# Moving the group-0 scores of a dilated attention layer six chunks later in its period

## The chip, the cores and the metric

The kernel runs on one core of a Trainium2 chip. The core has five engines with queues of their own: TensorE (PE in the profile, with its weight loads as PEld), VectorE (DVE), ScalarE (ACT), GpSimd (POOL) and SyncE (SP, which here only issues DMAs). They share the on-chip memory SBUF; PE writes its sums into the eight banks of PSUM, from which DVE and ACT read. The metric is the device time of one execution in microseconds. Times are medians of several runs; a profile is one more execution, recorded instruction by instruction.

## The reference

The program is a two-layer encoder trunk over 512 tokens of 1024 features, in float32. Layer 0 is a windowed attention, layer 1 a dilated one; each is followed by a SwiGLU feed-forward block. The change lies in layer 1's attention:

```python
DILATED_GROUPS = ((128, 1), (512, 4), (2048, 16))   # (window, dilation)

def dilated_mixture_attention(h, w_qkv, w_out):
    qkv = (h @ w_qkv).reshape(b, s, N_GROUPS_B, 3, H_B, HEAD_DIM)
    for gi, (win, dil) in enumerate(DILATED_GROUPS):
        q, k, v = (to_residue(qkv[:, :, gi, i], dil) for i in range(3))
        o, lse = banded_attention(q, k, v, slopes, dil, win // (2 * dil), BLOCK_B)
        outs.append(from_residue(o)); lses.append(from_residue(lse))
    wts = softmax(stack(lses), axis=0)
    o = einsum('gbsh,gbshd->bshd', wts, stack(outs))
    return o.reshape(b, s, H_B * HEAD_DIM) @ w_out
```

Each of 16 heads has queries, keys and values of its own in each of three groups. A group's scores are scaled, biased by distance, masked to a band, put through a softmax and multiplied with the values; the groups' results are then weighted by their softmax denominators and added.

## The kernel before

**Products.** A float32 operand is split into a high and a low part of the type that PE multiplies fast (ACT copies the high part, DVE subtracts it from the operand, lines 92 to 94), and a product is made of three: high by high, high by low, low by high (`mm3`, line 117). Weights are split in the same way when they arrive, `wh` by ACT and `wl` by DVE, in tiles of three buffers.

**Fillers.** Layer 1 needs, for each pair of heads (p from 0 to 7) and each group (0, 1, 2), a unit of queries, a unit of keys and a share of values. These products have few dependencies and are used as filling: the generator `fillers` (line 1276) lines all of them up, and each `next(fill)` issues one **chunk**, which is always six products of 128x256 (one eighth of a query or key unit, one sixteenth of a value unit). A unit of queries or keys is eight chunks in one of the three PSUM banks `mm`; at its end DVE scales it into SBUF (lines 1006 and 1017). For group 0 the result is split further: `split_queries` (line 129) makes the tiles `qs`, `split_keys` (line 134) the tiles `ks` and `kl`, with copies on ACT (lines 136, 137, 139) and a subtraction on DVE (line 138).

In each pair's period of 64 chunks the fillers come in this order: queries and keys of groups 1 and 2 of pair p (four units, 32 chunks), group 0's queries of pair p+1 (8), a unit of values (16), group 0's keys of pair p+1 (8). Pair 0 has 16 chunks more, a further unit of values ahead of the queries of pair 1. `spread([4], fill)` ahead of the loop lets the fillers run four chunks ahead, so that the keys of group 0 for pair p are over four chunks before the period of pair p begins.

**Attention.** Between the chunks stand the steps of attention itself. For group 0 (`attention_a`):

- `scores_a` (line 1045) for query blocks 0 and 1, then for 2 and 3: eight products each into the two banks `sc` (line 1063), then the bias, mask and maximum on DVE (line 1071) and the exponential on ACT (line 1076).
- `merge` (line 1187): POOL sends the softmax statistics to DRAM with two DMAs and reads them back in another order with four (lines 1192 to 1198).
- `turn_a` (line 1079), once per query block: PE transposes the probabilities into a bank `tp`; ACT or DVE copies them to SBUF (`evacuate`).
- `weigh`, called **the burst** here: without a chunk in between, PE issues the value products of groups 1 and 2 of the pair before (`finish`, line 1177, whose sum DVE adds at line 1183), those of group 0 of this pair (`weigh_a`, lines 1100 and 1104), and the scores of groups 1 and 2 (`scores_b`, line 1122). `scores_b` brings DVE work (lines 1135 to 1150), exponentials on ACT (line 1142) and a scaling on POOL (line 1154).

After the burst `attention_b` gives two transposes of groups 1 and 2 (`turn_b`, line 1164) and the merging rows (line 1204).

**Order.** PE's order is the order of the program (line 70: a schedule by hand for PE). In this layer the order of the other engines' instructions is laid out by the planner when the program is built, and each engine then works strictly in it.

**Where the steps stand.** `weave` (line 157) spreads `total` chunks evenly over the list that `attention_a` returns; a number in that list counts as a step of its own (and asks for that many chunks besides, here 0). The list has 13 entries, so entry i stands after `total * i // 13` chunks. With 32 chunks (pairs 1 to 7) the steps stand after 0 (first scores), 4 (second scores), 9 (merge), 12, 14, 17 and 22 (transposes) and 29 chunks (burst); three chunks more follow. With 48 chunks (pair 0) they stand after 0, 7, 14, 18, 22, 25, 33 and 44 chunks; four more follow. Then come 13 chunks, `first` (the transposes of the burst's first half), 8 chunks, `second`, 4 chunks, `rows`, 7 chunks. In the last pair it is 8 chunks, `first`, 5 chunks, `second`, `rows`, 2 chunks, and the fillers of its second half are parts of the output projection (`out_part`).

Of the kernel before, what the change touches and what calls it, by code (L numbers as in the profile page):

```python
# [66 lines left out]
def trunk(ctx, tc, xT, gains, sink, tabs, qsc, wunits, wv, outT, outR):  # L67
# [10 lines left out]
    def bank(tag, name=None):  # L78
        return psum.tile([128, 512], F32, tag=tag, name=name or tag, bufs=BUFS[tag])
# [73 lines left out]
    def chain(*gens):  # L153
        for _, g in gens:
            yield from g

    def weave(main, fill, total):

        done = 0
        for i, step in enumerate(main):  # L160
            want = total * (i + 1) // len(main)
            spread([step, want - done], fill)
            done = want

    def spread(main, fill):

        for step in main:
            if callable(step):
                step()
            else:  # L170
                for _ in range(step):
                    next(fill)
# [158 lines left out]
    with tc.tile_pool(name="l0", bufs=2) as pool:  # L331
# [7 lines left out]
        def k_unit(P, **kw):  # L339
            def done(ps):  # L340
                t = spool.tile([128, S], F32, name="tmp")
                nc.vector.tensor_tensor(t, ps, norm["rb"], op=OP.mult)
                qk["k", P] = [pool.tile([128, S], F32R, name=f"kt{a}") for a in range(2)]
                qk["kl", P] = [pool.tile([128, S], F32R, name=f"kl{a}") for a in range(2)]
                split_keys(t, qk["k", P], qk["kl", P])
            return unit(5 * P, xh, xl, "mm", done, **kw)

        def q_unit(P, i, **kw):
            def done(ps):
                t = spool.tile([128, S], F32, name="tmp")  # L350
                col = 4 * P + i
                nc.vector.scalar_tensor_tensor(t, ps, qs_sb[:, col:col + 1], norm["rb"], op0=OP.mult, op1=OP.mult)
                qk["q", P, i] = apart(pool, any(k[0] == "q" for k in qk), lambda: [
                    pool.tile([128, S], F32R, name=f"qt{a}", bufs=8) for a in range(2)])
                split_queries(t, qk["q", P, i])
            return unit(5 * P + 1 + i, xh, xl, "mm", done, **kw)
# [96 lines left out]
        def out_part(j, lo, hi, w={}):  # L453
            def gen():
                if lo == 0:
                    w[j] = load_unit(wunits[10 + j], (NK, 128))
                    out_ps[j] = bank("mm")
                wh, wl = w[j]
                for c in range(lo, hi):
                    mm3(out_ps[j], wh[:, c], wl[:, c], oh[:, c, :], ol[:, c, :], c == 0, c == NK - 1)  # L460
                    if c == NK - 1:
                        residual(j, out_ps[j], 1)
                    yield
            return hi - lo, gen()
# [4 lines left out]
        fill = chain((16, early), q_unit(0, 2), q_unit(0, 3), k_unit(1),  # L469
                     *[q_unit(1, i) for i in range(4)],  # L470
                     *[out_part(j, 0, 4) for j in range(3)], *[out_part(j, 4, 6) for j in range(3)])
# [509 lines left out]
    with tc.tile_pool(name="l1", bufs=2) as pool:  # L981
# [58 lines left out]
        def tile_a(t):  # L1040


            return 256 * (t % 2), 256 if t else 128

        def scores_a(p, ts):
            if ts[0] == 0:

                st["sta", p] = pool.tile([128, 4, 4], F32, name="sta")
            sta = st["sta", p]
            ps = [bank("sc") for a in range(2)]  # L1050
            pr = st["pr", p, ts] = pool.tile([128, 2, 512], F32, name="pr1", bufs=2)
            for t in ts:
                o = tile_a(t)[0]
                for a in range(2):
                    out, kp = ps[a][:, o:o + 256], [qk[n, p][a] for n in ("ks", "kl")]
                    if t == 0:

                        out = out.rearrange("p (b k) -> p b k", b=2)
                        kp = [k.rearrange("p (b k) -> p b k", b=4)[:, 0::3, :] for k in kp]
                    else:  # L1060
                        kp = [k[:, 128 * t - 128:128 * t + 128] for k in kp]
                    for k in range(2):
                        nc.tensor.matmul(out, qk["qs", p][a][:, 128 * t:128 * t + 128], kp[k],  # L1063
                                         start=t == ts[0] and k == 0, stop=k == 1, skip_group_check=True)
            for t in ts:
                o, n = tile_a(t)
                mx = pool.tile([128, 2], F32, name="mx1", bufs=4)
                for a in range(2):
                    for rows, at, tb in ((slice(0, 128), o, taba),) if t else ((HALVES[0], o + 128, tabe),
                                                                              (HALVES[1], o, tabe)):  # L1070
                        nc.vector.tensor_tensor_reduce(
                            out=pr[rows, a, o:o + n], in0=ps[a][rows, at:at + n], in1=tb[rows],
                            scale=SLOPES[2 * p + a], scalar=-3e38, op0=OP.add, op1=OP.max, accum_out=mx[rows, a:a + 1])
                nc.vector.tensor_scalar(sta[:, t, 0:2], mx, -1.0, None, op0=OP.mult)
                for a in range(2):
                    nc.scalar.activation(pr[:, a, o:o + n], pr[:, a, o:o + n], AF.Exp, bias=sta[:, t, a:a + 1],
                                         accum_out=sta[:, t, 2 + a:3 + a])

        def turn_a(p, ts, t):
            o, n = tile_a(t)  # L1080
            nb = n // 128
            tp = bank("tp")
            for a in range(2):
                for kb in range(nb):
                    nc.tensor.transpose(tp[:, (nb * a + kb) * 128:(nb * a + kb) * 128 + 128],  # L1085
                                        st["pr", p, ts][:, a, o + 128 * kb:o + 128 * kb + 128], ident)
            pt = st["pt"] = pool.tile([128, 512], F32, name="pt1", bufs=8)
            evacuate(pt[:, :2 * n], tp[:, :2 * n], t)
            return pt
# [97 lines left out]
        def merge(p):  # L1187


            sta = st["sta", p]  # L1190
            by_query = dram.tile([S + 64, 4], F32, name="stats")
            nc.gpsimd.dma_start(by_query[:S].rearrange("(t q) e -> q t e", t=4), sta)
            nc.gpsimd.dma_start(by_query[S:], sta[:64, 0, :])

            sa = st["sa", p] = pool.tile([128, 4, 4], F32, name="sa")
            by_class = by_query[64:].rearrange("(m c i) e -> i m c e", c=4, i=4)
            for i in range(4):
                nc.gpsimd.dma_start(sa[32 * i:32 * i + 32], by_class[i])
# [9 lines left out]
        def attention_a(p):  # L1208

            pts = {}  # L1210

            def turn(ts, t):
                pts[t] = turn_a(p, ts, t)

            def weigh():

                if p:
                    finish(p - 1)
                for t in range(4):
                    weigh_a(p, t, pts[t])  # L1220
                scores_b(p, (0, 1))
                scores_b(p, (2, 3))

            return [lambda: scores_a(p, (0, 1)), 0, lambda: scores_a(p, (2, 3)), 0,
                    lambda: merge(p), lambda: turn((0, 1), 0), lambda: turn((0, 1), 1),
                    lambda: turn((2, 3), 2), 0, lambda: turn((2, 3), 3), 0, 0, weigh]

        def attention_b(p):
            def turn(cs):
                st["pts", p, cs[0]] = turn_b(p, cs)  # L1230

            return [lambda: turn((0, 1)), lambda: turn((2, 3)), lambda: merge_rows(p)]

        def finish(p):
            for c in range(4):
                weigh_b(p, c, st["pts", p, c // 2 * 2])
# [58 lines left out]
        fill = fillers()  # L1295
        spread([4], fill)
        for p in range(8):
            weave(attention_a(p), fill, 48 if p == 0 else 32)
            first, second, rows = attention_b(p)
            if p < 7:  # L1300
                spread([13, first, 8, second, 4, rows, 7], fill)
# [99 lines left out]
```

## Time and profile before

| | us |
|---|---|
| runs | 1426.27, 1424.46, 1425.81 |
| median | 1425.81 |
| profiled execution | 1426.05 |
| its span, first to last instruction | 1424.3 |

| engine | busy us | share of the span |
|---|---|---|
| DVE | 857.0 | 60% |
| ACT | 683.5 | 48% |
| POOL | 232.0 | 16% |

Layer 1's attention with its fillers lies between about 582 and 1042 us of the span. A row of a timeline gives the start, the duration, engine, line, operation, and what is written and read (out<-in); a number in square brackets is the idle time of the engine just before, with the instruction that ended it. A row of a window gives the stretch, its length, the busy time and count of PE, PEld, DVE, ACT and POOL, then the granted share of PE's clock, the busy share of the DMA engines and GB/s. The busy time of a product on PE includes a tail that the next product overlaps, so that a chain of products is measured from start to start.

### The profile page before, as it was taken

To read this page: it belongs to the slowest core of one execution; us is meant where nothing else is said; L and a number is where in the kernel's file an instruction comes from. 1 tells how busy PE (TensorE), PEld (TensorE's weight loads), DVE (VectorE), ACT (ScalarE), POOL (GpSimd) and SP (SyncE) were. 2 spreads that over 40 slices of the span, in tenths; PEclk is the share of its full clock that TensorE was granted. 3 is DMA by queue.
4 is the path that set the end of the run, shared out by engine and by line. 5 is a ranking of instruction groups with operands and counts; after the bars stand their busy time and mean duration, and the time that the engine had idled before them with its cause. 6 is when DMAs were issued, how large, how long until landed. Compare 5 with 4: busy or idle time off the path is not lost. (4 is left out here: it accounts for less than half of the span.)

```text
span 1424.3 us, 29674 instructions
## 1 busy us (share of the span) xinstructions
PE 1398.5 (98%) x12418; PEld 1377.5 (97%) x12418; DVE 857.0 (60%) x1581; ACT 683.5 (48%) x1247; POOL 232.0 (16%) x325
## 2 busy tenths in 40 slices
PE   8999999999999999999999999999999999999998
PEld 8898999999999999999999999999999999999998
DVE  6776568843786373445554555546556884478733
ACT  6776434632565265344544445445443463256522
POOL 4334220100110120111121101111122010011022
PEclk9999999999999999999999999999999999999999
DMA  6110262833772232322122222122126284378121
GB/s 199 60 46 31 90 178 90 216 112 117 202 191 65 96 110 90 105 72 93 61 76 75 75 76 75 61 90 75 61 89 178 90 209 116 121 196 197 65 97 71
DMA packets 60486, 153.62 MB, mean 108 GB/s; under 512 B 8256, under 2 KB 13632, under 8 KB 60352
## 3 DMA queue, kind: packets, MB, share of 16 engines
q1 hardware_dynamic: 49168, 134.26, 28.3%
q0 software_dynamic: 10752, 16.92, 7.5%
q8 instruction: 97, 1.59, 0.4%
q10 hardware_dynamic: 432, 0.54, 0.1%
q14 instruction: 37, 0.30, 0.1%
HBM read 149.52 MB, written 2.17 MB: 107 GB/s over the span
## 5 line engine op out<-in xcount | busy, mean ns | idle before, releaser
L94 DVE TENSOR_TENSOR wl<-wraw,wh 128x1024 fp32r<-128x1024 f32 (+4 forms) x192 | 214.2, 1119 | 174.6 <-ACT wh L93 173.1
L93 ACT ACTIVATE wh<-wraw 128x1024 fp32r<-128x1024 f32 (+4 forms) x192 | 181.3, 949 | 265.2 <-PE mm L122 165.2
L122 PE MATMUL mm<-xh,wh 128*128 128x256 f32 x1320 | 270.6, 285 | 1.1 <-ACT wh L93 1.1
L122 PE MATMUL mm<-xh,wl 128*128 128x256 f32 x1320 | 263.2, 280 | 2.1 <-DVE wl L94 2.1
L122 PE MATMUL mm<-xl,wh 128*128 128x256 f32 x1320 | 263.1, 280 | 0.0
L122 PEld LDWEIGHTS mm<-xh,wh 128*128 128x128 f32 x1320 | 204.0, 191 | 3.7 <-issue 1.5
L122 PEld LDWEIGHTS mm<-xh,wl 128*128 128x128 f32 x1320 | 203.2, 191 | 2.7 <-DVE wl L94 2.5
L122 PEld LDWEIGHTS mm<-xl,wh 128*128 128x128 f32 x1320 | 203.4, 191 | 0.0
L653 POOL DMA_DIRECT2D w<-wunits x64 | 56.0, 917 | 416.5 <-DMA w<-wunits 111.9
L255 POOL TENSOR_TENSOR ssum<-ssum,tmp 128x512 f32<-128x512 f32 x33 | 54.1, 1639 | 191.9 <-ACT tmp L252 129.9
L122 PE MATMUL psv<-wh,xh 128*128 128x256 f32 x288 | 81.1, 281 | 0.0
L122 PE MATMUL psv<-wh,xl 128*128 128x256 f32 x288 | 80.3, 279 | 0.0
L122 PE MATMUL psv<-wl,xh 128*128 128x256 f32 x288 | 80.2, 279 | 0.0
L696 PE MATMUL mm<-bh,wh 128*128 128x256 f32 x256 | 70.7, 276 | 0.0
L696 PE MATMUL mm<-bl,wh 128*128 128x256 f32 x256 | 70.7, 276 | 0.0
L696 PE MATMUL mm<-bh,wl 128*128 128x256 f32 x256 | 70.7, 276 | 0.0
L696 PE MATMUL sc<-bh,wh 128*128 128x256 f32 x256 | 70.7, 276 | 0.0
L696 PE MATMUL sc<-bl,wh 128*128 128x256 f32 x256 | 70.7, 276 | 0.0
L696 PE MATMUL sc<-bh,wl 128*128 128x256 f32 x256 | 70.7, 276 | 0.0
L696 PE MATMUL mm<-bh,h 128*128 128x256 f32 x256 | 70.7, 276 | 0.0
L696 PE MATMUL mm<-bl,h 128*128 128x256 f32 x256 | 70.7, 276 | 0.0
L696 PE MATMUL mm<-bh,l 128*128 128x256 f32 x256 | 70.7, 276 | 0.0
(240 smaller groups left out, 3718.6 us busy)
## 6 DMA issues: line engine op xcount, KB each, us to landing
wraw<-wunits SPq DMA_DIRECT2D x159, 512.0 KB, 3.3
w<-wunits SPq DMA_DIRECT2D x96, 256.0 KB, 4.3
w<-wunits POOLq DMA_DIRECT2D x64, 256.0 KB, 5.8
wraw<-wv SPq DMA_DIRECT2D x25, 512.0 KB, 3.3
wraw<-wunits SPq DMA_DIRECT2D x28, 192.0 KB, 2.4
x<-xT SPq DMA_DIRECT2D x8, 256.0 KB, 4.9
wraw<-wunits SPq DMA_DIRECT2D x4, 256.0 KB, 4.9
wraw<-wunits SPq DMA_DIRECT2D x2, 384.0 KB, 2.9
```

The lines of the kernel that those rows point to most:

```text
L93: nc.scalar.activation(out_h, src, AF.Copy)
L94: nc.vector.tensor_tensor(out_l, src, out_h.bitcast(F32), op=OP.subtract)
L122: nc.tensor.matmul(out[:, cols], a, b[:, cols], start=first and k == 0 and c == 0, stop=last and k == 2, skip_group_check=True)
L255: nc.gpsimd.tensor_tensor(norm["sum"], norm["sum"], sq, op=OP.add)
L653: nc.gpsimd.dma_start(sums[:, 512 * k:512 * k + 512], v[:, 0:512], accum_op=OP.add)
L696: nc.tensor.matmul(out, a[:, j], b[:, j], start=first and j == 0 and i == 0, stop=j == 3 and i == 2, skip_group_check=True)
```

## The change

The spreading by `weave` is replaced by numbers of chunks written into the list. They are 6 chunks (22 for pair 0) ahead of the first scores, and then 4, 5, 2, 2, 4, 3 and 6.

```diff
-            return [lambda: scores_a(p, (0, 1)), 0, lambda: scores_a(p, (2, 3)), 0,
-                    lambda: merge(p), lambda: turn((0, 1), 0), lambda: turn((0, 1), 1),
-                    lambda: turn((2, 3), 2), 0, lambda: turn((2, 3), 3), 0, 0, weigh]
+            return [lambda: scores_a(p, (0, 1)), 4, lambda: scores_a(p, (2, 3)), 5,
+                    lambda: merge(p), 2, lambda: turn((0, 1), 0), 2, lambda: turn((0, 1), 1), 4,
+                    lambda: turn((2, 3), 2), 3, lambda: turn((2, 3), 3), 6, weigh]
...
         for p in range(8):
-            weave(attention_a(p), fill, 48 if p == 0 else 32)
+
+            spread([6 if p else 22, *attention_a(p)], fill)
             first, second, rows = attention_b(p)
```

The steps of pairs 1 to 7 then stand after 6 (first scores), 10 (second scores), 15 (merge), 17, 19, 23 and 26 (transposes) and 32 chunks (burst). Those of pair 0 stand after 22, 26, 31, 33, 35, 39, 42 and 48. The sum is 32 or 48 as before, so that `first`, `second` and `rows` keep their places among the chunks. Between burst and `first` there are now 13 chunks (16 before in pairs 1 to 6, 17 in pair 0), and 8 in the last pair (11 before). The burst itself is not divided.

## The prediction

> **What bounds the kernel now.** I read the page's busy times first, then the waits of PE, then the timeline of PE at the place that the waits name, then windows cut by period, and last the timelines of the engines that PE waits for.
>
> ```profile
> span 1424.3 us, 29674 instructions
> ## 1 busy us (share of the span) xinstructions
> PE 1398.5 (98%) x12418; PEld 1377.5 (97%) x12418; DVE 857.0 (60%) x1581; ACT 683.5 (48%) x1247; POOL 232.0 (16%) x325
> ```
>
> PE is the bound: no other engine passes 60%. A change that only moves PE's work about can gain only where PE waits or runs at a lower clock. The two longest entries in the waits of PE (us in total, times, longest) are these:
>
> ```profile
> PE sc L1063 <- ACT kl L139: 7.2, 12, 0.9
> PE sc L1063 <- ACT ks L137: 3.0, 7, 0.4
> ```
>
> L1063 is the score product of group 0, the step that is moved. It waits for the key copies of `split_keys` seven times: in heads pairs 1 to 7, not in pair 0. The entries add up to 10.2 us, but the timeline of PE shows that more is lost. Pair 1:
>
> ```profile
> 646.12 0.39 PE L122 MATMUL mm<-xh,wl 128*128 128x256 f32 x2
> 646.93 0.38 PE L1063 MATMUL sc<-ks,qs 128*128 128x256 f32 x1 [0.43 <-ACT ks L137]
> ...
> 649.59 0.39 PE L122 MATMUL mm<-xh,wh 128*128 128x256 f32 x2
> ...
> 652.31 0.28 PE L1063 MATMUL sc<-ks,qs 128*128 128x256 f32 x1
> ...
> 653.22 0.39 PE L122 MATMUL mm<-xh,wh 128*128 128x256 f32 x2
> ```
>
> Product starts count here, since each product's tail overlaps the next. Between 649.59 and 652.31 lie four chunks (24 products), so a **chunk takes 0.68 us** and one product 0.113 us. The second scores take 653.22 - 652.31 = 0.91 us with nothing to wait for. The pair that starts at 646.12 lets the next product start at 646.35; the first eight scores should be over at 647.26 and are at 649.59. **One stall costs 2.33 us**, 0.58 of it ahead of the first score product and 1.75 behind it. The rest of the idle time hides in products whose busy time is stretched.
>
> The windows from one pair's first score to the next pair's (length, busy times, then the granted clock third from the end) show a second loss:
>
> ```profile
> 646.93:703.51 56.58, 55.07 (x523) 54.05 (x523) 31.63 (x79) 26.48 (x61) 8.47 (x14) 1.00 0.23 76
> 703.51:761.68 58.17, 56.69 (x523) 55.67 (x523) 31.61 (x79) 26.57 (x61) 8.46 (x14) 0.97 0.23 74
> 761.68:819.84 58.16, 56.66 (x522) 55.65 (x522) 31.62 (x79) 26.59 (x61) 8.46 (x14) 0.97 0.23 74
> 819.84:878.34 58.50, 57.00 (x522) 55.98 (x523) 31.73 (x79) 26.58 (x61) 8.46 (x14) 0.97 0.23 74
> 878.34:934.91 56.57, 55.07 (x523) 54.06 (x523) 31.63 (x79) 26.47 (x61) 8.46 (x14) 1.00 0.23 76
> 934.91:993.07 58.16, 56.66 (x522) 55.64 (x522) 31.61 (x79) 26.57 (x61) 8.47 (x14) 0.97 0.22 74
> ```
>
> Same work, but 58.16 us at clock 0.97 against 56.57 at 1.00: **1.59 us more**. Finer windows find the half clock right behind the stall, in pairs 2, 3, 4, 6 and 7 (first and last of the five):
>
> ```profile
> 705.80:709.22 3.42, 3.42 (x19) 3.42 (x18) 2.20 (x14) 1.11 (x5) 0.00 (x0) 0.50 0.00 0
> ...
> 995.94:999.35 3.41, 3.41 (x18) 3.41 (x17) 1.96 (x14) 1.80 (x8) 0.57 (x1) 0.50 0.01 2
> ```
>
> Their distance, 290.14 us, is 85 times 3.413, so the stretches sit on a fixed grid. Pair 1's stall (646.35 to 649.59, less the products in it) and pair 5's straddle a line of that grid (647.78, 879.88) and have no half clock; the five others lie inside one cell and have one. So I book the half clock to the stall.
>
> **The change part by part.** *The stall.* The next pair's keys end with the last chunk of their unit, then go through DVE and ACT:
>
> ```profile
> 643.40 0.39 PE L122 MATMUL mm<-xh,wl 128*128 128x256 f32 x2
> ...
> 643.83 1.07 DVE L1017 TENSOR_TENSOR ka<-mm,rb 128x512 f32<-128x512 f32 x1 [1.36 <-PE mm L122]
> ...
> 647.56 1.28 ACT L139 ACTIVATE kl<-kl 64x512 fp32r<-64x512 f32 x2
> ```
>
> The unit is over at 643.62, the last copy at 648.84: 5.22 us. Today four chunks (2.73 us) stand between unit and scores, after the change ten: 10 x 0.68 = 6.8 us. The stall goes, with 1.6 us to spare. Pair 0 has none to lose; there the scores move from chunk 0 to chunk 22, and all its distances become those of the other pairs.
>
> Sum: a clean period is 56.57 - 2.33 = 54.24. The six windows add up to 346.14; six clean ones are 325.44, a gain of 20.70. Outside them lie 0.58 (before pair 1's first score) and, in pair 7, 1.75 and 1.59 of half clock: 3.92. Together **24.6 us**.
>
> [...]
>
> *What moves and keeps its cover.* No instruction is added or taken away. PE issues the same products, DVE, ACT and POOL the same operations, and `merge` the same six DMAs on POOL's queue; SP's weight loads stay where they are among the chunks. What changes is distances in chunks. First scores to their first transposes: 12 to 11; second scores to theirs: 13 to 13; last transposes to the burst: 7 to 6; end of the second group's keys to the burst: 1 to 4, a relief. The waits of PE name no transposes or values of this layer today, so a shortened distance costs at most what it shrinks, 0.68 us; I take nothing, since 11 chunks (7.5 us) and 6 chunks (4.1 us) stand there.
>
> `merge` moves with the scores; from the second scores to the burst 25 chunks become 22. The last issue ends at 660.29 + 2.23 = 662.52, and the reader stands at 678.06:
>
> ```profile
> 660.29 2.23 POOL L1198 DMA_DIRECT2D sa<-stats  x4 [1.99 <-DMA stats<-sta]
> ...
> 678.06 0.16 DVE L1138 SCALAR_TENSOR_TENSOR mb<-mb,sa 128x4 f32<-128x4 f32 x1
> ```
>
> 15.5 us less 2.04 leave 13.5 for the landing: nothing.
>
> *The second half of the scores* takes the two `sc` banks that DVE reads for the first half:
>
> ```profile
> 649.56 0.29 DVE L1071 CUSTOM_DVE_ANT_0 pr<-sc,tab 64x128 f32<-64x128 f32 x1 [2.31 <-PE sc L1063]
> ...
> 651.25 0.42 DVE L1071 CUSTOM_DVE_ANT_0 pr<-sc,tab 128x256 f32<-128x256 f32 x1
> ```
>
> DVE reads 2.1 us, beginning about 0.3 us after the first score, and the banks are wanted 0.91 + 2.72 = 3.6 us after it. Today DVE is idle and waits for PE; after the change the scores come two chunks after a query unit ends, whose scaling and the next weights' split may stand in front. Those take 1.17 + 1.38 = 2.55 us after that unit by the rows below (an estimate, the longest forms), that is until 2.55 - 1.36 = 1.2 us after the first score, so the banks are free at about 3.3 of 3.6 us: nothing, but only 0.3 us from a wait.
>
> *The burst* comes at chunk 32 instead of 29, and what follows it stays where it was. So whatever the burst feeds loses 3 chunks, 2.04 us. The third value product lies in the bank of the query unit, which DVE empties (qa) behind the burst's softmax:
>
> ```profile
> 683.81 1.17 DVE L1006 SCALAR_TENSOR_TENSOR qa<-mm,qs_sb,rb 128x448 f32<-128x448 f32 x2
> 684.84 1.38 DVE L94 TENSOR_TENSOR wl<-wraw,wh 128x1024 fp32r<-128x1024 f32 x1
> ...
> 687.89 0.28 PE L122 MATMUL psv<-wh,xh 128*128 128x256 f32 x1
> ```
>
> The bank is free at 684.98 and wanted at 687.89; 2.91 - 2.04 leaves 0.87 us: nothing. In the last pair only 8 chunks stay between burst and transposes:
>
> ```profile
> 1028.99 1.97 POOL L1154 TENSOR_SCALAR pr<-pr,mb 128x256 f32<-128x256 f32 x4 [16.88 <-DVE mb L1147]
> ...
> 1032.70 0.60 PE L1164 MATMUL tp<-ident,pr 128*128 128x128 f32 x4
> ```
>
> POOL ends at 1030.96, 1.74 us early; 1.74 - 2.04 = -0.3. Waiting for three chunks less, **PE loses up to 0.3 us**; I take 0.2. In the other pairs 13 chunks stay, five more, 3.4 us of cover. Net: 24.6 - 0.2 = **24.4 us**.
>
> The profiled execution took 1426.05 us (span 1424.3 and 1.75 around it); 1426.05 - 24.4 = 1401.65. The median of the runs, 1425.81, lies 0.24 below that execution: **1401.4 us**.
>
> **The rivals.** *Late DVE work binds behind the burst.* PE's order is written out, DVE's is laid by the planner. Should it put the weight split (1.38) ahead of qa, the third value product waits 1.38 - 0.87 = 0.5 us in seven pairs, 3.6 us: 1405; the worst I can bound is the full 2.04 in seven pairs, 14.3 us: 1415.7. For: the spare time shrinks from 2.9 to 0.9. Against: the query unit now ends nearer to the burst, while DVE still waits for ACT's exponentials, so qa may also go earlier.
>
> *The half clock stays.* Then only the stalls go: 7 x 2.33 - 0.2 = 16.1, 1409.7. [...] Against: five of five begin within the stall's cell, and no other place of the stage has one.
>
> *The change doesn't do what it says.* If the planner puts key copies back as far as the scores went, 4.1 us, PE stalls as before: 1425.8. That needs three more weight splits ahead of them; the copies are due in the same place as before.
>
> *Slower.* The wait goes to the `sc` banks of the second scores. With 0.3 us to spare, each further us of DVE work ahead of the first half's reading costs PE a us in all eight pairs. To come out slower by 0.2% it takes (24.4 + 2.9) / 8 = 3.4 us each, so DVE 3.7 us late: three weight splits of 1.2 to 1.4 us in a row, or one that stands in DVE's queue waiting for weights. Then 1428.7. If such a wait brings the half clock too (1.59), 2.1 us of lateness are enough. Against it: a unit needs one split, not three.
>
> **How the numbers follow.** Forecast 1401.4, chance 0.72 (1398 to 1404). Late DVE work (1405 to 1416) 0.12, half clock stays 0.05, slower 0.04, does nothing 0.03; 0.04 for more gain than I found or a mixture. Low end 1398: one window of equal work and clock took 58.50 against 58.16 for no cause that I name; 0.34 in eight pairs, 2.7 us, may come or go. High end 1411: beyond the second rival and the cheaper half of the first. A measurement of this kernel can tell about 0.2% (2.9 us) from no change. Faster 0.72 + 0.12 + 0.05 + 0.03 = 0.92; same 0.04; slower 0.04.
>
> **What would show it.** Right: no wait of L1063 for ACT in the waits of PE; granted clock 1.00 in every window of the stage; periods of 54.2 us; in the last pair's first transposes a wait for POOL of at most 0.3 us. Wrong: a wait of value products for DVE qa, of L1063 for DVE L1071, stretches of half clock without a stall, or periods of 56 us and more.

## The result and the profile after

| | before | after |
|---|---|---|
| median of five runs, us | 1425.98 | 1401.90 |
| lowest to highest, us | 1424.46 to 1426.74 | 1401.66 to 1403.02 |
| profiled execution, us | 1426.05 | 1401.66 |
| mean granted clock of its span | 0.992 | 0.999 |

The ratio is 0.9834, with a 95% interval of 0.9819 to 0.9848. The two profiled executions differ by 24.39 us.

The page of the changed kernel, then the head of its waits of PE (us in total, times, longest):

```profile
span 1399.9 us, 29676 instructions
## 1 busy us (share of the span) xinstructions
PE 1385.8 (99%) x12418; PEld 1368.5 (98%) x12418; DVE 857.9 (61%) x1581; ACT 683.0 (49%) x1247; POOL 237.6 (17%) x325
```

```profile
PE mm L122 <- DVE wl L94: 1.6, 3, 0.8
PE warm L316 <- POOL ident masks.py:199: 1.4, 1, 1.4
```

The five engines' counts of instructions are those of before. The two lines of L1063 that led the waits are gone; what leads now lies outside the heads pairs. The windows from one pair's first score to the next, cut as before:

```profile
649.49:703.72 54.23, 54.23 (x524) 53.81 (x523) 32.04 (x79) 26.50 (x60) 9.34 (x14) 1.00 0.25 79
703.72:757.96 54.24, 54.24 (x525) 53.82 (x523) 32.05 (x79) 26.50 (x60) 9.32 (x14) 1.00 0.23 79
...
920.66:974.89 54.23, 54.23 (x524) 53.81 (x523) 32.05 (x79) 26.50 (x60) 9.34 (x14) 1.00 0.24 79
```

All six last 54.23 or 54.24 us at the full clock, and PE's busy time fills each of them. They add up to 974.89 - 649.49 = 325.40 us where they were 346.14. That is 20.74 of the 24.39 us; the other 3.65 us lie ahead of the first window and behind the last, and are taken apart below.

The timelines of PE, DVE and ACT where pair 1 waited before:

```profile
642.46 0.39 PE L122 MATMUL mm<-xh,wl 128*128 128x256 f32 x2
...
649.26 0.39 PE L122 MATMUL mm<-xh,wl 128*128 128x256 f32 x2
649.49 0.28 PE L1063 MATMUL sc<-ks,qs 128*128 128x256 f32 x1
...
650.40 0.39 PE L122 MATMUL mm<-xh,wh 128*128 128x256 f32 x2
```

```profile
642.89 1.07 DVE L1017 TENSOR_TENSOR ka<-mm,rb 128x512 f32<-128x512 f32 x1 [1.37 <-PE mm L122]
```

```profile
646.61 1.29 ACT L139 ACTIVATE kl<-kl 64x512 fp32r<-64x512 f32 x2
```

The key unit is over at 642.69 and its last copy at 647.90, 5.21 us later, as before. The first score starts at 649.49, 1.59 us after that copy, straight behind the product before it, and the eight scores take 0.91 us. The copies are not faster; PE has other work until they are there.

### The profile page after: what moved, and what is told of

It reads as the page before. It is cut to its first block, busy times and chain, and to the rows that moved or that the text cites. A ratio compares the mean times of both kernels' runs of the same rounds, so it can differ in the third digit from the quotient of the medians.

```text
span 1399.9 us, 29676 instructions
## 1 busy us (share of the span) xinstructions
PE 1385.8 (99%) x12418; PEld 1368.5 (98%) x12418; DVE 857.9 (61%) x1581; ACT 683.0 (49%) x1247; POOL 237.6 (17%) x325
## 3 DMA queue, kind: packets, MB, share of 16 engines
q8 instruction: 97, 1.59, 0.5%
## 4 chain that ended last, share of the span: by engine, by line
PE 96%; DVE 1%; ACT 1%; issue 0%; DMA 0%; SPq 0%; POOL 0%; DVEq 0%; ACTq 0%
PE mm L122 40%; PE mm L696 12%; PE sc L122 11%; PE psv L122 10%; PE sc L696 9%; PE tp L122 5%; PE ov L413 1%; PE sc L144 1%; PE tp L400 1%; PE sc L1122 1%; PE ovb L1177 1%; PE sc L1063 1%; PE tp L1085 1%; PE ov L1104 1%; PE tp L1164 1%
## 5 line engine op out<-in xcount | busy, mean ns | idle before, releaser
L122 PE MATMUL mm<-xh,wh 128*128 128x256 f32 x1320 | 267.6, 283 | 0.9 <-ACT wh L93 0.9
L122 PE MATMUL mm<-xl,wh 128*128 128x256 f32 x1320 | 260.3, 277 | 0.0
L122 PEld LDWEIGHTS mm<-xh,wh 128*128 128x128 f32 x1320 | 201.0, 188 | 3.9 <-issue 1.5
L122 PEld LDWEIGHTS mm<-xh,wl 128*128 128x128 f32 x1320 | 200.4, 188 | 1.6 <-DVE wl L94 1.6
L122 PEld LDWEIGHTS mm<-xl,wh 128*128 128x128 f32 x1320 | 200.6, 188 | 0.0
```

The lines of the kernel that those rows point to most:

```text
L122: nc.tensor.matmul(out[:, cols], a, b[:, cols], start=first and k == 0 and c == 0, stop=last and k == 2, skip_group_check=True)
```

## The experiments

The edits are against the changed kernel where not said otherwise. Each batch ran beside the kernel before on the same chip, and its ratio is to that one.

**The burst alone moved.** Scores, merge and transposes stand where they stood before, the burst after 32 chunks (48 in pair 0).

```diff
-            spread([6 if p else 22, *attention_a(p)], fill)
+            spread([0 if p else 0, *attention_a(p)], fill)
```

with the numbers in the list 4, 5, 3, 2, 3, 5, 10 (pair 0: 7, 7, 4, 4, 3, 8, 15).

> Scores, merge and transposes where they were before the change (after 0, 4, 9, 12, 14, 17 and 22 chunks), the burst alone at its new place, 32 chunks. Theory (the whole gain is the wait of the first scores for the key copies, and the half clock that it brings): the time of before, 1426 us, with seven waits of 2.33 us at L1063. Rival (the gain is the burst's, which now comes four chunks after the second group's keys instead of one): about 1402 us, the stalls at L1063 no longer costing what I counted. A split between the two would show as a time in between.

Measured: 1424.99 us, ratio 1.0008 (0.9993 to 1.0023): no difference. The waits of PE have L1063 back in full:

```profile
PE sc L1063 <- ACT kl L139: 7.4, 13, 0.9
PE sc L1063 <- ACT ks L137: 3.0, 7, 0.4
```

So the new place of the burst earns nothing.

**The scores moved, the burst back.** The burst stands after 29 chunks (45 in pair 0), three chunks follow it.

```diff
-                    lambda: turn((2, 3), 2), 3, lambda: turn((2, 3), 3), 6, weigh]
+                    lambda: turn((2, 3), 2), 3, lambda: turn((2, 3), 3), 3, weigh, 3]
```

> Scores, merge and transposes at their new places, the burst back at 29 chunks. Theory: 1401.7 us, the time of the change less 0.14 us in the last pair, whose first transposes have three chunks more again. Rival (the burst's place carries the gain): 1426 us; a split shows in between.

Measured: 1400.89 us, ratio 0.9832 (0.9817 to 0.9848). The whole gain comes with the scores, the merge and the transposes behind them.

**Early keys.** Against the kernel before: the scores stay where they were, and the keys of the next pair's group 0 come ahead of the values.

```diff
-                    line += [v[0], q, v[1], k]
+                    line += [v[0], q, k, v[1]]
...
-                    line += [q, v[1], k]
+                    line += [q, k, v[1]]
...
-                    line += [q, lambda pg=pg, **kw: v_unit(pg + 1, 1, **kw), k]
+                    line += [q, k, lambda pg=pg, **kw: v_unit(pg + 1, 1, **kw)]
```

> The order of before, but in the line of fillers the next pair's group-0 keys stand ahead of the values instead of behind them, so that the keys are over 20 chunks ahead of the first scores instead of 4. Theory: the same gain without moving the scores, 1401.5 to 1403 us, no wait at L1063, clock 1.00, periods of 54.2 us. Rival (the gain comes from where the scores stand among the fillers, not from the keys' age): 1426 us or a part of the gain only.

Measured: 1404.45 us (1403.10 to 1404.86), ratio 0.9855 (0.9840 to 0.9871). No wait at L1063, and the granted clock is 1.00 in the two periods from 646.51 to 755.76. So the age of the keys is the cause: making them older by another way, with the scores at chunk 0, gives most of the gain, 19.3 us against the 1423.74 of its batch, where the scores-only version gained 22.9. The time lies above the expected 1401.5 to 1403 us, though. A window and the rows of PE's timeline ahead of it show why:

```profile
701.13:755.76 54.63, 54.63 (x525) 54.21 (x524) 31.75 (x79) 26.40 (x60) 8.46 (x14) 1.00 0.24 79
```

```profile
694.26 0.28 PE L122 MATMUL psv<-wh,xl 128*128 128x256 f32 x1
...
695.62 0.28 PE L122 MATMUL psv<-wh,xl 128*128 128x256 f32 x1
695.74 0.60 PE L1204 MATMUL rrow<-ident,ew 128*128 128x128 f32 x4
...
696.30 0.28 PE L122 MATMUL psv<-wl,xh 128*128 128x256 f32 x1
...
698.30 0.40 PE L122 MATMUL mm<-xh,wh 128*128 128x256 f32 x2
```

The period is 0.4 us longer than in the changed kernel, with PE busy throughout, because some of its products run at a slower pace. Ahead of the merging rows (L1204) 12 products take 1.36 us from start to start, 0.113 each; behind them 17 products, from 696.30 to 698.30, take 2.00 us, 0.118 each, 4% more. So the slower pace begins behind the four transposes of the merging rows, still among the value products; it goes on through the switch to query products at 698.30, to the group of four transposes at 713.13.

**A lead of 1, 2 and 3 chunks instead of 6.** The first scores of pairs 1 to 7 come earlier by so many, and the second scores and all else stay (shown for 2).

```diff
-            return [lambda: scores_a(p, (0, 1)), 4, lambda: scores_a(p, (2, 3)), 5,
+            return [lambda: scores_a(p, (0, 1)), 8 if p else 4, lambda: scores_a(p, (2, 3)), 5,
...
-            spread([6 if p else 22, *attention_a(p)], fill)
+            spread([2 if p else 22, *attention_a(p)], fill)
```

> The changed kernel with the first scores of pairs 1 to 7 after 2 chunks instead of 6, the rest as in the change. Theory: six chunks (4.1 us) stand between keys and scores, so each stall shrinks by 2 x 0.68 to 0.97 us, seven of them 6.8 us: 1408.7 us if stalls of 1 us don't bring the half clock; if they bring it as the long ones do, five times 1.59 more, 1416.7 us. Rival (half clock independent of the stall): 1408.7 us exactly as the first case, but with stretches of half clock in places without a stall.

> The changed kernel with the first scores of pairs 1 to 7 after 1 chunk instead of 6. Theory: each stall is 5 x 0.68 us shorter cover than needed by 1.65 us, seven of them 11.6 us over the changed kernel, about 1413 us if a stall of 1.65 us leaves the clock alone, and 1.6 us more for every stretch of half clock that it brings (at most seven, 1424 us). Rival (the stall has a fixed price once the scores come too early): 2.33 us each again, about 1418 us without half clock. Whether half clock comes says where between 0.97 us (none seen) and 2.33 us (four or five of seven) it sets in.

> The changed kernel with the first scores after 3 chunks instead of 6. Theory: seven chunks, 4.76 us, stand between keys and scores, 0.29 us short by the straight line 2.33 - 0.68 a chunk (0.97 at 2 and 1.65 at 1 were on it): seven times 0.29, 2.0 us, 1403.6 us. Rival (the second and later key copies, not the first, set the wait near the end of the line, so it bends): 1401.6 us, no wait.

Measured, with the changed kernel of the same or the nearest batch (1401.55 and 1402.67 us):

| chunks ahead of the scores | time, us | over the changed kernel | one stall, us | seven stalls | half clock in the profile |
|---|---|---|---|---|---|
| 0 (the kernel before) | 1425.98 | 24.1 | 2.33 | 16.3 | 5 times |
| 1 | 1413.32 | 11.8 | 1.65 | 11.6 | none |
| 2 | 1407.60 | 6.1 | 0.97 | 6.8 | none |
| 3 | 1405.53 | 2.9 | 0.30 | 2.1 | none |
| 6 (the changed kernel) | 1401.90 | 0 | 0 | 0 | none |

The stall with a lead of 1 is the length of its period, 55.88 us, less 54.23; with 2, 55.21 less 54.23 (0.98, and 0.97 by product starts):

```profile
646.86:702.74 55.88, 54.81 (x525) 53.99 (x523) 32.04 (x79) 26.36 (x61) 9.33 (x14) 1.00 0.23 76
```

```profile
645.91:701.12 55.21, 54.80 (x524) 53.98 (x523) 31.83 (x78) 26.37 (x61) 9.34 (x14) 1.00 0.26 78
```

With a lead of 3 the eight scores run from 648.21 to 649.41, 1.20 us instead of 0.91:

```profile
648.21 0.28 PE L1063 MATMUL sc<-ks,qs 128*128 128x256 f32 x1
...
649.41 0.40 PE L122 MATMUL mm<-xh,wh 128*128 128x256 f32 x2
```

Each chunk takes its 0.68 us off the stall, on a straight line down to 0.3; the fixed price is refuted, and so is the bend. (With a lead of 3 the waits of PE have no entry of L1063 at all: the 0.30 us show in the starts alone.) The times with a lead of 1 to 3 follow the seven stalls within 0.8 us; without a lead the half clock comes on top, 7.8 us by the table, where five stretches of 1.59 us make 7.95. The 0.8 us of the lead of 3 fit the slower pace again: three of its six periods last 54.96 to 54.99 us, the other three 54.52 or 54.53.

**The second scores 2 chunks behind the first.**

```diff
-            return [lambda: scores_a(p, (0, 1)), 4, lambda: scores_a(p, (2, 3)), 5,
+            return [lambda: scores_a(p, (0, 1)), 2, lambda: scores_a(p, (2, 3)), 7,
```

> The changed kernel with the second scores 2 chunks behind the first instead of 4, merge and transposes staying. Theory (the score banks are free about 2.5 us after the first score, the first of them, and 2.9 us, the second; wanted now 2.27 us after it): a wait of about 0.5 us at the second scores in all eight pairs, 4 us, 1405.9 us, named in the waits of PE as L1063 for DVE L1071. Rival (DVE hides it by reading ahead of its other work): 1401.9 us and no such wait.

Measured: 1407.60 us, 6.1 above the changed kernel beside it. The waits of PE name a new one in eight pairs:

```profile
PE sc L1063 <- DVE sta L1074: 2.3, 8, 0.3
```

From product start to product start it costs 0.74 us in pairs 1 to 7 and 0.68 in pair 0, 5.9 us together. The mechanism is the one I gave for the slower rival, in another size. (The named instruction is the one after the last reading of L1071.)

**Early keys, with the merging rows 4 chunks later.** Against the early-keys kernel:

```diff
-                spread([13, first, 8, second, 4, rows, 7], fill)
+                spread([13, first, 8, second, 8, rows, 3], fill)
```

> The kernel with early keys (scores unmoved, keys ahead of values) took 1404.45 us, with periods of 54.62 us against 54.23 and no wait: its products start 0.118 us apart instead of 0.113 from the switch from value products to query products on, until a group of four transposes. Here the merging rows (four transposes) come 4 chunks later, one chunk after that switch. Theory (four transposes end the slower pace): some 130 products a period run at 0.113 again, periods of about 54.0 us, 1400.2 us, a little under the changed kernel. Rival (the pace belongs to the order of units, not to what stands between): 1404.4 us as before.

Measured: 1403.38 us (1402.27 to 1404.46); the changed kernel beside it took 1401.55. The first two windows:

```profile
646.31:700.41 54.10, 54.10 (x525) 53.68 (x523) 31.77 (x78) 26.36 (x60) 8.47 (x14) 1.00 0.24 79
700.41:754.94 54.53, 54.53 (x524) 54.11 (x523) 31.67 (x78) 26.41 (x60) 8.46 (x14) 1.00 0.24 79
```

The expectation took the slower pace to begin at the switch from value products to query products. In the early-keys kernel it does so in the first period (at 643.69); in the second it begins behind the merging rows, as in the rows above. With the rows moved it begins at the switch in the second period (697.15), and the four transposes one chunk behind (697.85) do not end it: from 698.52 to 700.41 16 products still take 1.89 us, 0.118 each. In the first period, where it had begun earlier, they do (54.10 us against 54.53). So the theory held in the first period and fell in the second, and what sets the pace stays open.

**The changed kernel and the version with the burst back, once more.**

> The changed kernel itself, as the yardstick for the three that run beside it: 1401.9 us, periods of 54.23 us, no wait at L1063.

> The changed kernel again, as the yardstick on this chip: 1401.6 us.

> Scores moved, burst back at 29 chunks, beside the changed kernel on the same chip. Theory: 0.14 us in the last pair's first transposes is all that the later burst costs, so 1401.5 us, no difference that can be measured. Rival (the later burst costs more than that, as 1400.9 us against 1401.6 in earlier runs may hint): 0.6 us or more below the changed kernel.

Measured: the changed kernel 1401.55 us in the one batch and 1402.67 (1402.42 to 1403.24) in the other; beside the latter the scores-only version took 1401.19 (1399.74 to 1401.75), ratio 0.9828 (0.9813 to 0.9842). It is the fastest that was tried, 1.5 us (0.1%) below the changed kernel beside it. So the theory (0.14 us, no difference that can be measured) fell, and the rival's number came; but most of it is no wait that the burst's place makes. The stretch from the last pair's last value products to the end, in the changed kernel and in the scores-only version, holds the same instructions in the same order on PE:

```profile
1013.57:1399.90 386.33, 378.60 (x3333) 377.35 (x3332) 239.74 (x333) 169.30 (x248) 57.77 (x57) 0.99 0.47 132
```

```profile
1012.62:1398.00 385.38, 377.67 (x3333) 376.42 (x3332) 239.75 (x333) 169.29 (x248) 57.87 (x57) 0.99 0.47 132
```

It is 0.95 us longer in the changed kernel. The output projection in it runs at the slower pace there (282 products from 1021.74 on, 0.118 apart), and at the faster one in the scores-only version:

```profile
1033.75 0.40 PE L122 MATMUL mm<-oh,wh 128*128 128x256 f32 x2
...
1035.87 0.40 PE L122 MATMUL mm<-oh,wh 128*128 128x256 f32 x2
```

```profile
1033.07 0.39 PE L122 MATMUL mm<-oh,wh 128*128 128x256 f32 x2
...
1035.33 0.39 PE L122 MATMUL mm<-ol,wh 128*128 128x256 f32 x2
```

Between these rows lie 18 products in 2.12 us, 0.118 each, and 20 in 2.26 us, 0.113 each. The lead-3 kernel, with the burst as late as in the change, also has the shorter stretch (1018.19 to the end at 1403.5, 385.3 us), so the burst's place alone doesn't bring it. The one wait that the later burst adds is in the last pair's first transposes, 0.13 us.

## Why the prediction was right

**The stall** was named and sized rightly: 5.22 us of key copies against four chunks, 5.21 measured after. Burst alone and scores alone put the whole gain on the scores; early keys show that it is the keys' age, and the leads of 1, 2 and 3 give the straight line.

**The half clock** went with the stalls, as booked: none of the six windows shows less than 1.00. Of the seven stalls of the burst-alone kernel four were followed by it in the profiled execution, and none of the 21 shorter stalls of the lead kernels, whose spans have the changed kernel's mean clock of 0.999. The rival by which it stays would have given 1409.7; it is refuted.

**The sum**, 24.4 us, came out at 24.39 between the profiled executions, and clean periods, put at 54.24, are 54.23. What the sum counts was right: the windows (20.74), the wait ahead of the first (0.58), and stall and half clock in pair 7 (3.35, from its first score to the last value product of its burst, less three chunks) make 24.67 for the 24.6 forecast. But that the total agrees to 0.01 is luck, since two things that the sum leaves out cancel. Pair 1's key unit was over at 642.69 instead of 643.62, 0.93 us earlier and ahead of every stall. That is chance: in a repeat of the changed kernel DVE takes the unit up at the same time as in the kernel before.

```profile
643.83 1.09 DVE L1017 TENSOR_TENSOR ka<-mm,rb 128x512 f32<-128x512 f32 x1 [1.37 <-PE mm L122]
```

Against it, from the last pair's first transposes to the end the changed kernel needs 1.22 us more, not 0.2: 0.13 in the transposes, and the rest from the slower pace behind them, most of it in the output projection. It mattered, too, which execution of the kernel before was profiled: single ones lie between 1420.70 and 1427.84 us. By the medians the gain is 24.1, 24.1 and 22.5 us in the three batches with the changed kernel.

The window of 58.50 us, whose 0.34 us the forecast could not name, is the slower pace as well: the second scores in it, from 826.86 to 827.80, take 0.94 us instead of 0.91, and the products behind them run 0.118 apart until a group of four transposes at 835.10. By an estimate from these rows some 80 products lose about 0.4 us so.

**The last pair** was put at 0.2, at most 0.3. POOL ends at 1007.44, and the four transposes take 0.74 us instead of 0.60 (0.49 instead of 0.36 to the start of the next product, 0.13 lost):

```profile
1005.47 1.97 POOL L1154 TENSOR_SCALAR pr<-pr,mb 128x256 f32<-128x256 f32 x4 [15.01 <-DVE mb L1147]
```

```profile
1007.08 0.74 PE L1164 MATMUL tp<-ident,pr 128*128 128x128 f32 x4
```

**The third value product** has more room than I gave it. I left 0.87 us on the assumption that DVE's order stays. DVE now empties the query bank earlier:

```profile
679.90 0.42 DVE L1150 TENSOR_TENSOR ew<-mb 128x256 f32<-128x256 f32 x1
680.24 1.18 DVE L1006 SCALAR_TENSOR_TENSOR qa<-mm,qs_sb,rb 128x448 f32<-128x448 f32 x2
```

```profile
684.61 0.28 PE L122 MATMUL psv<-wh,xh 128*128 128x256 f32 x1
```

qa stands between the burst's two softmax halves, in the time in which DVE had waited for ACT's exponentials, and ends at 681.42, 3.2 us before the bank is wanted. The planner went the way that I had named as the reason against that rival.

**The score banks** have 0.65 us to spare, not 0.3:

```profile
648.33 0.75 DVE L1006 SCALAR_TENSOR_TENSOR q<-mm,qs_sb,rb 128x512 f32<-128x512 f32 x1 [2.01 <-PE mm L122]
649.20 1.23 DVE L94 TENSOR_TENSOR wl<-wraw,wh 128x1024 fp32r<-128x1024 f32 x1
...
652.05 0.42 DVE L1071 CUSTOM_DVE_ANT_0 pr<-sc,tab 128x256 f32<-128x256 f32 x1
```

The last reading ends at 652.47; the second scores start at 650.40 + 2.72 = 653.12. The scaling and the split do stand in front of the reading, but I had priced the scaling by the longer group-0 form, 1.17 us, where it takes 0.75. The gap of two chunks says the same by another way: 1.36 us closer cost 0.74, so 0.62 had been free.

**The merge** leaves 11.7 us for the landing (last issue over at 662.87 + 2.23 = 665.10, reader at 676.82) where I had 13.5, because the chain from the second scores to that issue took 11.98 us instead of 10.21; nothing waits for it.

```profile
662.87 2.23 POOL L1198 DMA_DIRECT2D sa<-stats  x4 [3.31 <-DMA stats<-sta]
```

```profile
676.82 0.16 DVE L1138 SCALAR_TENSOR_TENSOR mb<-mb,sa 128x4 f32<-128x4 f32 x1
```

## What to carry to other kernels

Where one engine is busy throughout, measure a wait from start to start: the list of waits gave 10.2 us, the starts 16.3, and the clock cost 8 more. The wait for a chain of copies was cured here by age, with copies as slow as before, since other work could stand in between. For a wait of this kind, work out the chain's length, then put the consumer that many products later, or the producer earlier, and look at what the moved step comes close to next. When a forecast agrees to the last digit, check its parts as well: here the parts were right, and the last digit was not earned.

## What the runs showed of the hardware

**When the half clock set in.** The grid cells of 3.41 us around the stalls, each followed by its neighbour; first the kernel before, pair 5, then the burst-alone kernel, pairs 4 and 5, then the lead-1 kernel, pair 2 (its grid is laid by the half clock at the end of its span, at 1409.0). The second column is the length, the third PE's busy time with the count of products:

```profile
876.47:879.88 3.41, 2.06 (x16) 1.67 (x14) 2.17 (x3) 3.29 (x6) 0.00 (x0) 1.00 0.41 149
879.88:883.30 3.42, 3.26 (x28) 3.06 (x28) 2.20 (x14) 0.85 (x4) 0.00 (x0) 1.00 0.01 5
```

```profile
819.28:822.69 3.41, 1.96 (x13) 1.36 (x11) 1.81 (x3) 3.29 (x6) 0.00 (x0) 1.00 0.48 154
822.69:826.10 3.41, 3.36 (x15) 3.36 (x16) 2.20 (x14) 0.45 (x4) 0.00 (x0) 0.50 0.02 5
877.30:880.72 3.42, 2.06 (x14) 1.46 (x12) 1.90 (x3) 3.30 (x6) 0.00 (x0) 1.00 0.39 151
880.72:884.13 3.41, 3.27 (x28) 3.27 (x29) 2.20 (x14) 0.85 (x5) 0.00 (x0) 1.00 0.01 2
```

```profile
702.46:705.87 3.41, 2.33 (x18) 1.93 (x17) 1.10 (x5) 2.02 (x4) 0.00 (x0) 1.00 0.47 159
705.87:709.29 3.42, 3.42 (x33) 3.42 (x32) 2.33 (x11) 2.17 (x9) 0.57 (x1) 1.00 0.00 0
```

Around the stalls of the kernel before and the burst-alone kernel, the nine cells that a half-clock cell follows hold 1.90 to 1.96 us of PE's busy time, 12 or 13 products; the lowest without consequence hold 2.06 us, 14 or more products. So a cell need not be idle: behind these nine, over half of each busy by this count, the next one ran at a granted clock of 0.50. (The count includes the products' tails; in the kernel before 9 to 12 products start in such a cell, where 30 fit at 0.113 us.) No limit in busy time follows from it: elsewhere in the kernel before the cell from 12.90 to 16.31 holds 1.93 us, 17 products, and is followed by a clock of 1.00, the one from 1415.78 to 1419.19 holds 2.02 us, 17 products too, and is followed by 0.50. The same stall passed without half clock when a grid line cut it, twice of seven times in the kernel before and three times in the burst-alone kernel. All the runs of the kernel before spread from 1420.70 to 1427.84 us, at a granted clock of 0.990 to 0.996, those of the changed kernel from 1401.03 to 1403.24. By an estimate the 7.14 us are four or five half-clock stretches of 1.59 us; what makes the spread was not shown.

**Two paces.** PE's products run 0.113 or 0.118 us apart at the same granted clock, 1.00, for dozens of products on end. The slower pace cost 0.40 us a period in the early-keys kernel (54.63 against 54.23) and 0.95 us from the last value products to the end of the changed kernel (386.33 against 385.38), as much as the smaller differences between the kernels here. In the changed kernel seven stretches of it begin with the first value product behind a query product and end, 54 products later, at the four transposes of L1164 (in pair 1 at 678.96 and 685.33); the kernel before has six of these. But in the early-keys kernel it begins behind the merging rows, four transposes too (695.74; 0.118 apart from 696.30 on), and in the run that relied on transposes those at 697.85 did not end it. What sets the pace stays open.
